# A hybrid RG-LRU / Conformer layer on one core: RMS row, gate and LayerNorm matmuls moved by a quarter or two, a fifth landing place for the squares of x, mean differences in small buffers

## The chip, the core and the metric

The kernel runs on one core of a Trainium2 chip. Its metric is device time in microseconds (us), median of three runs. TensorE (PE) does the matmuls, VectorE (DVE) and ScalarE (ACT) work on tiles in on-chip memory, GpSimd (POOL) and SyncE (SP) mostly issue transfers.

## What is computed

One layer over 1088 tokens (1024 of a prompt, 8 x 8 of a decode batch), all in float32:

```python
proj = rmsnorm(x) @ w_in                  # 2048 -> 5 x 1024
xa, ga, vb, gglu, gb = split(proj)
xc = dwconv4(xa)                          # causal, then block-diagonal gates
r, ig = sigmoid(xc @ gate_a + b), sigmoid(xc @ gate_x + b)
a = exp(-8 * r * softplus(-lru_param))
h = scan(a, sqrt(1 - a*a) * ig * xc)      # h[t] = a[t] h[t-1] + b[t]
ya = h * silu(ga)
u = vb * sigmoid(gglu)
yb = silu(layernorm(dwconv31(u))) * silu(gb)
y = rmsnorm(x + concat(ya, yb) @ w_out)   # and states h, conv tails
```

## The kernel before

Every float32 operand of a matmul is split into a rounded part `hi` and a rest `lo`, and each product is three matmuls (hi·hi, lo·hi, hi·lo). The projection runs over 40 column blocks of 128, in the `order` gg, vb, xa, ga for each of eight channel groups i (n = 4i to 4i+3), and then the eight gb blocks (n = 32 to 39). The first two blocks run together while x arrives, in eight units (`project_unit`, two values of k for both blocks). From n = 2 on, `project` runs a block in four quarters q of four values of k, one unit each. A unit is 32 matmuls. Each unit's weights are loaded by SP, split by ACT (L159) and DVE (L160) two units ahead, in a ring of three buffers.

`at(n, q, f)` puts f behind the unit of quarter q of block n (q of 4 and more counts on into later blocks), so f's matmuls stand in PE's queue there. Each engine's queue has a fixed order, written at build time by a planner that goes by place in the program: `tc.high_priority(URGENT)` moves the weight splits up by 200, `pump` moves the 31 taps of the long convolution (L412 to L416) and the mean update `stats` back by 400. An instruction whose input is late holds up all behind it on its engine.

The normalisation of x is folded in after the projection. `square_x` loads x by POOL into one of four borrowed places (two of tag "wmq", one "cb", one "sg") and ACT squares it, 18 times; `rms_stats` makes 1/rms, spreads it over a diagonal, splits that, and five pairs of small matmuls with ones (L363, L364) give the row `rstd`, which ACT copies out (L365). Blocks of n = 2 on need `rstd` to leave PSUM: `a_half` (xa), `first_b` (the first two blocks, parked in on-chip memory), `scaled`. PSUM has eight banks; a block takes three, a gate chunk two, each piece of the RMS row one.

For group i, `a_half` convolves xa in three chunks (`conv`, at the quarters `A_CONV`) and `a_chunk` runs six gate matmuls per chunk (at `A_GATE`). These use a ring of nine small buffers, `tt`. The product with silu(ga) goes to DRAM from a "sg" buffer, of which there are two. `stats` keeps a running mean of the long convolution's output over the groups: the difference `wd` goes into a "sg" buffer too, and `add_squares` squares it. In n = 33 and 34, `ln_mean` and `ln_rstd` sum over partitions with ones (L316, L317); `finish_b` applies the LayerNorm. The output projection follows.

Of the kernel before, what the change touches and what calls it, by code (L numbers as in the profile page):

```python
# [7 lines left out]
F32 = mybir.dt.float32  # L8
F32R = mybir.dt.float32r
# [20 lines left out]
LRU_C = 8.0  # L30
EPS = 1e-6

A_CONV = (0, 1, 3)
A_GATE = (2, 4, 6)
WARM = 8
URGENT = 200
LATER = 400
LN_AT = (0, 4, 6)
TAPS = {"xa": 3, "ga": 1, "gg": 2, "vb": 2}


# [22 lines left out]
def hybrid_layer_kernel(  # L64
# [135 lines left out]
    def project_unit(g, pts):  # L200

        hi, lo = wsplit.pop(g)
        wide, part, rest = [], [], []
        for m, (n, k) in enumerate(units[g]):
            ks = slice(m * P, (m + 1) * P)
            first, last = k == 0, k == NK - 1
            xh, xl = xs_[k]
            for src, w_t, fl, ll in ((xh, hi, first, False), (xl, hi, False, False), (xh, lo, False, last)):
                for c, (t0, tn, gr, go) in enumerate(CHUNKS[:2]):
                    to = wide if c == 0 else part  # L210
                    to.append((w_t is lo, pts[n][c][:, :tn], w_t[:, ks], src[gr][:, go : go + tn], fl, ll))

            t0, tn, gr, go = CHUNKS[2]
            both = xg_[k].rearrange("p (s t) -> p s t", s=2)[:, :, go : go + tn]
            pt = pts[n][2]
            wide.append(
                (False, pt[:, : 2 * tn].rearrange("p (s t) -> p s t", s=2), hi[:, ks], both, first, False)
            )
            rest.append((True, pt[:, :tn], lo[:, ks], xh[gr][:, go : go + tn], False, last))
        for group in (wide, part, rest):  # L220
            for _, out, w, mv, fl, ll in sorted(group, key=lambda z: z[0]):
                PE.matmul(out, w, mv, start=fl, stop=ll)  # L222

# [74 lines left out]
    squares = []  # L298

    def add_squares():  # L300
        for m, d in squares:
            S.activation(d, d, AF.Square, scale=float((m / (m + 1.0)) ** 0.5))
            V.tensor_add(wmq[1], wmq[1], d)
        squares.clear()

    def at(n, q, f):
        hooks.setdefault((n + q // NQ, q % NQ), []).append(f)


    def partition_sum(pt, src, c, name):  # L310

        t0, tn = ACH[c]
        hi, lo = tt(f"{name}h{c}", F32R), tt(f"{name}l{c}", F32R)
        S.copy(hi[:, :tn], src)
        V.tensor_sub(lo[:, :tn], src, hi[:, :tn].bitcast(F32))
        PE.matmul(pt[:, :tn], ones_r, hi[:, :tn], start=True, stop=False)  # L316
        PE.matmul(pt[:, :tn], ones_r, lo[:, :tn], start=False, stop=True)  # L317

    def square_x(n):

        t0, h = n // 2 * P, n % 2
        m = min(P, T - t0)

        if n % 4 < 2:
            xt = sp.tile([P, T], F32, tag="wmq", name=f"xt{n}", bufs=2)
        else:
            xt = full(*((("cb", f"xt{n}", 1), ("sg", f"xt{n}", 2))[n % 4 - 2]))
        if n < 2:

            G.tensor_copy(xt[:, :1], xs_[NK - 2 + n][0][0][:, :1].bitcast(F32))  # L330
        G.dma_start(xt[:m, : D // 2], x[t0 : t0 + m, h * (D // 2) : (h + 1) * (D // 2)])
        c = h * NT + n // 2
        S.activation(xt[:m, : D // 2], xt[:m, : D // 2], AF.Square, accum_out=ssx[:m, c : c + 1])

    def rms_stats():

        v, r, t = (sp.tile([P, NT], F32, name=f"rms{m}") for m in range(3))
        V.tensor_tensor(v, ssx[:, :NT], ssx[:, NT:], ALU.add)
        V.tensor_scalar(v, v, 1.0 / D, EPS, ALU.mult, ALU.add)
        S.activation(r, v, AF.Sqrt)  # L340
        V.reciprocal(r, r)
        refine(r, v, t)

        for n in range(0, NT, 2):
            t0 = n * P
            tn = min(2 * P, T - t0)
            c, o = divmod(t0, 512)
            nb = -(-tn // P)
            w = min(tn, P)
            dg, hi, lo = tt(f"dg{n}"), tt(f"dh{n}", F32R), tt(f"dl{n}", F32R)  # L350
            G.affine_select(
                out=dg[:, :tn].rearrange("p (b t) -> p b t", t=w),
                in_=r[:, n : n + nb].unsqueeze(2).to_broadcast([P, nb, w]),
                pattern=[[0, nb], [1, w]],
                base=0,
                channel_multiplier=-1,
                compare_op=ALU.is_equal,
                fill=0.0,
            )
            S.copy(hi[:, :tn], dg[:, :tn])  # L360
            V.tensor_sub(lo[:, :tn], dg[:, :tn], hi[:, :tn].bitcast(F32))
            pt = bank(f"rb{n}")
            PE.matmul(pt[:, :tn], ones_r, hi[:, :tn], start=True, stop=False)  # L363
            PE.matmul(pt[:, :tn], ones_r, lo[:, :tn], start=False, stop=True)  # L364
            S.copy(rstd[:, t0 : t0 + tn], pt[:, :tn])  # L365

    def full(tag, name, bufs):
        return ka.tile([P, T], F32, tag=tag, name=name, bufs=bufs)
# [34 lines left out]
    def b_conv(i, u, us):  # L403
        G.dma_start(o_bp[i], u[:, SEQ : SEQ + CB - 1])
        G.dma_start(o_bs[i].rearrange("p (b s) -> p b s", s=CB - 1), us[:, :, DS:])
        cb = full("cb", f"cb{i}", 1)
        cs = cb[:, SEQ:].rearrange("p (b s) -> p b s", s=DS)

        def tap(j):
            w = col(C_BW + j, i)  # L410
            if j == 0:
                V.tensor_scalar(cb[:, :SEQ], u[:, :SEQ], w, col(C_BB, i), ALU.mult, ALU.add)  # L412
                V.tensor_scalar(cs, us[:, :, :DS], w, col(C_BB, i), ALU.mult, ALU.add)
            else:
                V.scalar_tensor_tensor(cb[:, :SEQ], u[:, j : j + SEQ], w, cb[:, :SEQ], ALU.mult, ALU.add)  # L415
                V.scalar_tensor_tensor(cs, us[:, :, j : j + DS], w, cs, ALU.mult, ALU.add)  # L416

        def stats():
            G.dma_start(cbd[i], cb)
            wm, wq = wmq  # L420
            if i == 0:
                S.copy(wm, cb)
                G.memset(wq, 0.0)
                return
            d = full("sg", f"wd{i}", 2)
            V.tensor_sub(d, cb, wm)
# [131 lines left out]

    G.memset(ssx, 1.0)
    for n in range(2 * NT):  # L560
        at(2, n // 4, lambda n=n: square_x(n))
    at(2, 4, rms_stats)
    wmq = []
    at(2, 4, lambda: wmq.extend(sp.tile([P, T], F32, tag="wmq", name=f"wmq{m}", bufs=2) for m in range(2)))
    at(2, 2, softplus_consts)
    at(2, 6, first_b)

    conv = None
    for n, (kind, i, ct) in enumerate(order):
        if kind == "gb":  # L570
            break
        if n < 2:
            continue
        pts = project(n, TAPS[kind] if i < NC - 1 else 4)
        if kind == "gg":
            sg = full("sg", f"sg{i}", 2)
            scaled(sg, pts)
            b_gate(sg)
        elif kind == "vb":
            pump(len(bg))  # L580
            u, us = u_buffer(i)
# [47 lines left out]
    for n in range(4 * NC, 5 * NC):  # L629
        i = n - 4 * NC  # L630
        if i == 1:
            at(n, LN_AT[0], lambda: pump(len(bg)))
            at(n, LN_AT[0], add_squares)
            at(n, LN_AT[0], ln_mean)
            at(n, LN_AT[1], ln_rstd)
            at(n, LN_AT[2], lambda sg=sg0: finish_b(0, sg))
        if i > 1:
            at(n, LN_AT[2] - NQ, lambda i=i, sg=sg: finish_b(i - 1, sg))
        pts = project(n, 8)
        sg = full("sg", f"sgb{i}", 2)  # L640
        if i == 0:
# [266 lines left out]
```

## Time and profile before

| | |
|---|---|
| median of three runs | 1396.89 us (1396.36 to 1400.49) |
| the profiled execution | 1391.9 us |
| its span, first to last instruction | 1390.2 us |
| PE busy | 98% of the span |
| DVE busy | 69% |
| ACT busy | 39% |

The rows of the trace stand further below. Times are us from the start of the span. "Idle before <- releaser" is how long the engine stood still ahead of the instruction, and what ended that.

### The profile page before, as it was taken

The page shows a single profiled execution, that of the slowest core. Times are in us where ns is not written, and L with a number is a line of the kernel's source. Part 1 is how long each engine was busy: PE and PEld are TensorE (multiplying, and loading weights), DVE is VectorE, ACT ScalarE, POOL GpSimd, SP SyncE. Part 2 cuts the span into 40 slices and gives each one's busy share as a digit, 9 for nine tenths or more (in the row PEclk, how much of TensorE's full clock was granted, in tenths as well). Part 3 has the DMA queues.
Part 4 walks back from the last instruction along what each step waited for, and adds up shares of the span by engine and source line. Part 5 has one row for each costly group of instructions (what it writes and reads, how often), then busy time and mean ns, then how long its engine had stood idle before and what let it go on. Part 6 is the DMA issues. An engine that isn't in the chain of part 4 may idle for free.

```text
span 1390.2 us, 18376 instructions
## 1 busy us (share of the span) xinstructions
PE 1361.7 (98%) x6998; PEld 1185.9 (85%) x6998; DVE 954.1 (69%) x1625; ACT 546.4 (39%) x887; POOL 83.4 (6%) x153
## 2 busy tenths in 40 slices
PE   8989999999999999999999999999999999999997
PEld 7868888888888888888888898888888888888886
DVE  6359989798798796895996995843433463444342
ACT  6653617217227126126136164332333353333232
POOL 0210110100101001001001000000000000100000
PEclk9989999999999999999999999999999999999999
DMA  8831131321322313114123133343773356622333
GB/s 296 268 108 50 62 59 45 80 49 64 59 45 69 59 47 79 49 46 78 50 47 74 52 97 65 104 116 104 250 239 128 123 161 212 222 65 79 122 103 109
DMA packets 69129, 143.73 MB, mean 103 GB/s; under 512 B 9073, under 2 KB 12785, under 8 KB 68913
## 3 DMA queue, kind: packets, MB, share of 16 engines
q1 hardware_dynamic: 60032, 113.84, 28.0%
q0 software_dynamic: 8864, 28.72, 7.7%
q8 instruction: 54, 0.88, 0.3%
q14 instruction: 35, 0.28, 0.1%
q10 hardware_dynamic: 144, 0.01, 0.0%
HBM read 119.00 MB, written 23.54 MB: 103 GB/s over the span
## 4 chain that ended last, share of the span: by engine, by line
PE 58%; DVE 22%; ACT 7%; issue 6%; DMA 6%; POOL 1%; SPq 0%; DVEq 0%; ACTq 0%; POOLq 0%
PE pp L222 30%; DVE cb L415 9%; PE po L729 8%; PE po L728 8%; PE po L731 7%; DMA yd<-sga 3%; DVE wl L160 3%; DVE cb L416 3%; DMA xt<-in_x_dram 2%; DVE xc L464 2%; PE pz L729 1%; PE pz L728 1%; PE pz L731 1%; ACT L487 1%; ACT wh L159 1%
## 5 line engine op out<-in xcount | busy, mean ns | idle before, releaser
L222 PE MATMUL pp<-xg,wh 128*128 128x320 f32 (+1 forms) x1920 | 464.4, 336 | 1.9 <-DVE xg L194 1.9
L222 PEld LDWEIGHTS pp<-xg,wh 128*128 128x128 f32 x1920 | 321.7, 188 | 41.0 <-DVE xg L194 2.2
L415 DVE SCALAR_TENSOR_TENSOR cb<-u,prm,cb 128x1024 f32<-128x1024 f32 x240 | 307.1, 1280 | 1.6
L222 PE MATMUL pp<-xh,wh 128*128 128x512 f32 x640 | 252.7, 395 | 0.3 <-ACT xh L193 0.3
L222 PE MATMUL pp<-xl,wh 128*128 128x512 f32 x640 | 252.2, 394 | 0.3 <-DVE xl L194 0.3
L159 ACT CAST wh<-wr 128x512 fp32r<-128x512 f32 (+1 forms) x161 | 98.0, 612 | 279.8 <-DMA wr<-in_w_in_dram 130.0
L222 PE MATMUL pp<-xg,wl 128*128 128x256 f32 (+1 forms) x1280 | 196.3, 296 | 0.0
L222 PEld LDWEIGHTS pp<-xg,wl 128*128 128x128 f32 x1280 | 185.9, 189 | 0.0
L718 DVE TENSOR_TENSOR ol<-or,oh 128x512 fp32r<-128x512 f32 x114 | 78.5, 690 | 143.4 <-ACT oh L717 137.3
L222 PE MATMUL pp<-xh,wl 128*128 128x512 f32 x640 | 172.5, 391 | 1.0 <-DVE wl L160 0.9
L160 DVE TENSOR_TENSOR wl<-wr,wh 128x512 fp32r<-128x512 f32 (+1 forms) x161 | 109.9, 683 | 59.5 <-ACT wh L159 37.7
L222 PEld LDWEIGHTS pp<-xh,wl 128*128 128x128 f32 x640 | 119.5, 188 | 29.0 <-DVE wl L160 4.7
L222 PEld LDWEIGHTS pp<-xh,wh 128*128 128x128 f32 x640 | 121.8, 190 | 21.2 <-ACT xh L193 0.6
L222 PEld LDWEIGHTS pp<-xl,wh 128*128 128x128 f32 x640 | 121.6, 190 | 19.7 <-DVE xl L194 0.6
L717 ACT CAST oh<-or 128x512 fp32r<-128x512 f32 x114 | 70.6, 621 | 153.4 <-PE po L731 73.9
L729 PE MATMUL po<-ol,yh 128*128 128x512 f32 x256 | 99.8, 390 | 0.0
L728 PE MATMUL po<-oh,yh 128*128 128x512 f32 x256 | 99.7, 389 | 0.0
L731 PE MATMUL po<-oh,yl 128*128 128x512 f32 x256 | 99.7, 389 | 0.0
L729 PE MATMUL po<-ol,yg 128*128 128x512 f32 x240 | 93.6, 390 | 0.0
L728 PE MATMUL po<-oh,yg 128*128 128x512 f32 x240 | 93.5, 390 | 0.0
L731 PE MATMUL po<-oh,yg 128*128 128x512 f32 x192 | 74.8, 389 | 0.0
L416 DVE SCALAR_TENSOR_TENSOR cb<-u,prm,cb 128x64 f32<-128x64 f32 x240 | 67.7, 282 | 4.8
(217 smaller groups left out, 1466.2 us busy)
## 6 DMA issues: line engine op xcount, KB each, us to landing
wr<-in_w_in_dram SPq DMA_DIRECT2D x152, 256.0 KB, 3.0
or<-in_w_out_dram SPq DMA_DIRECT2D x128, 256.0 KB, 3.5
xt<-in_x_dram POOLq DMA_DIRECT2D x16, 512.0 KB, 5.5
xr<-in_x_dram SPq DMA_DIRECT2D x32, 256.0 KB, 3.1
xraw<-in_xT_dram SPq DMA_DIRECT2D x15, 544.0 KB, 6.1
yr<-yd SPq DMA_DIRECT2D x16, 288.0 KB, 2.8
cbd<-cb POOLq DMA_DIRECT2D x8, 544.0 KB, 3.9
yd<-sga POOLq DMA_DIRECT2D x8, 544.0 KB, 8.9
```

What stands on the lines that cost most here:

```text
L159: S.copy(hi[:, sl], raw[:, sl])
L160: V.tensor_sub(lo[:, sl], raw[:, sl], hi[:, sl].bitcast(F32))
L222: PE.matmul(out, w, mv, start=fl, stop=ll)
L415: V.scalar_tensor_tensor(cb[:, :SEQ], u[:, j : j + SEQ], w, cb[:, :SEQ], ALU.mult, ALU.add)
L416: V.scalar_tensor_tensor(cs, us[:, :, j : j + DS], w, cs, ALU.mult, ALU.add)
L464: V.scalar_tensor_tensor(o, src(j), col(C_AW + j, i), o, ALU.mult, ALU.add)
L487: S.activation(a[:, :tn], r[:, :tn], AF.Exp, scale=sp_n[:, i : i + 1])
L717: S.copy(hi, raw)
L718: V.tensor_sub(lo, raw, hi.bitcast(F32))
L728: PE.matmul(pt, yh, hi, start=k == 0, stop=False)
L729: PE.matmul(pt, yh, lo, start=False, stop=k == NK - 1 and yl is None)
L731: PE.matmul(pt, yl, hi, start=False, stop=k == NK - 1)
```

## The change

Six things. The quarters of the gate and LayerNorm work move: `A_CONV` (0, 1, 3) to (0, 1, 4), `A_GATE` (2, 4, 6) to (3, 5, 7), `LN_AT` from three places to five. The RMS row's matmuls leave `rms_stats` for `rms_row`, two quarters later, in three wide pieces where there were five; the diagonal and its split now live in "cb" and "wmq" buffers. `first_b` and the first `a_half` go a quarter later. The squares of x rotate through five places (the fifth is xa's buffer), five to a quarter. `stats` works on three chunks in `tt` buffers instead of one "sg" buffer. The first unit runs all of k = 0 ahead of k = 1. In LayerNorm, the split (`parts`) is issued a quarter ahead of the matmuls.

```diff
-A_CONV = (0, 1, 3)
-A_GATE = (2, 4, 6)
+A_CONV = (0, 1, 4)
+A_GATE = (3, 5, 7)
-LN_AT = (0, 4, 6)
+LN_AT = (0, 1, 3, 5, 7)
...
     def project_unit(g, pts):
-        wide, part, rest = [], [], []
-        for m, (n, k) in enumerate(units[g]):
+        blocks = list(enumerate(units[g]))
+        if g == 0:
+            for k in (0, 1):
+                project_blocks([b for b in blocks if b[1][1] == k], hi, lo, pts)
+        else:
+            project_blocks(blocks, hi, lo, pts)
...
-            wide.append(
+            (side if len(blocks) == 2 else wide).append(
...
-        for group in (wide, part, rest):
+        for group in (wide, side, part, rest):
...
     def add_squares():
-        for m, d in squares:
+        for m, d, sl in squares:
             S.activation(d, d, AF.Square, scale=float((m / (m + 1.0)) ** 0.5))
-            V.tensor_add(wmq[1], wmq[1], d)
+            V.tensor_add(wmq[1][:, sl], wmq[1][:, sl], d)
...
-        if n % 4 < 2:
+        m5 = n % 5
+        if m5 < 2:
             xt = sp.tile([P, T], F32, tag="wmq", name=f"xt{n}", bufs=2)
+        elif m5 < 4:
+            xt = full(*((("cb", f"xt{n}", 1), ("sg", f"xt{n}", 2))[m5 - 2]))
         else:
-            xt = full(*((("cb", f"xt{n}", 1), ("sg", f"xt{n}", 2))[n % 4 - 2]))
+            xt = kb.tile([P, AS + DB * AW], F32, tag="xa", name=f"xt{n}")
...
     def rms_stats():
+        dg = full("cb", "dg", 1)
+        dh, dl = (sp.tile([P, T], F32R, tag="wmq", name=f"d{m}", bufs=2) for m in "hl")
...
-            S.copy(hi[:, :tn], dg[:, :tn])
-            V.tensor_sub(lo[:, :tn], dg[:, :tn], hi[:, :tn].bitcast(F32))
-            pt = bank(f"rb{n}")
-            PE.matmul(pt[:, :tn], ones_r, hi[:, :tn], start=True, stop=False)
-            PE.matmul(pt[:, :tn], ones_r, lo[:, :tn], start=False, stop=True)
-            S.copy(rstd[:, t0 : t0 + tn], pt[:, :tn])
+            S.copy(dh[:, sl], dg[:, sl])
+            V.tensor_sub(dl[:, sl], dg[:, sl], dh[:, sl].bitcast(F32))
+        diag.extend((dh, dl))
+
+    def rms_row():
+        dh, dl = diag
+        for t0 in range(0, T, 512):
+            tn = min(512, T - t0)
+            sl = slice(t0, t0 + tn)
+            pt = bank(f"rb{t0}")
+            PE.matmul(pt[:, :tn], ones_r, dh[:, sl], start=True, stop=False)
+            PE.matmul(pt[:, :tn], ones_r, dl[:, sl], start=False, stop=True)
+            S.copy(rstd[:, sl], pt[:, :tn])
+        wmq.extend(sp.tile([P, T], F32, tag="wmq", name=f"wmq{m}", bufs=2) for m in range(2))
...
-            d = full("sg", f"wd{i}", 2)
-            V.tensor_sub(d, cb, wm)
-            V.scalar_tensor_tensor(wm, d, 1.0 / (i + 1), wm, ALU.mult, ALU.add)
-            squares.append((i, d))
+            for c, (t0, tn) in enumerate(ACH):
+                sl = slice(t0, t0 + tn)
+                d = tt(f"wd{i}_{c}")[:, :tn]
+                V.tensor_sub(d, cb[:, sl], wm[:, sl])
+                V.scalar_tensor_tensor(wm[:, sl], d, 1.0 / (i + 1), wm[:, sl], ALU.mult, ALU.add)
+                squares.append((i, d, sl))
...
-        at(2, n // 4, lambda n=n: square_x(n))
+        at(2, n // 5, lambda n=n: square_x(n))
     at(2, 4, rms_stats)
-    at(2, 4, lambda: wmq.extend(sp.tile([P, T], F32, tag="wmq", name=f"wmq{m}", bufs=2) for m in range(2)))
+    at(2, 6, rms_row)
     at(2, 2, softplus_consts)
-    at(2, 6, first_b)
+    at(2, 7, first_b)
...
-            at(n, 5, lambda n=n, i=i, pts=pts: a_half(n + 1, i, pts))
+            at(n, 6, lambda n=n, i=i, pts=pts: a_half(n + 1, i, pts))
...
-            at(n, LN_AT[0], ln_mean)
-            at(n, LN_AT[1], ln_rstd)
-            at(n, LN_AT[2], lambda sg=sg0: finish_b(0, sg))
+            at(n, LN_AT[0], lambda: ln_parts("lm", wm))
+            at(n, LN_AT[1], ln_mean)
+            at(n, LN_AT[2], lambda: ln_parts("lv", wq))
+            at(n, LN_AT[3], ln_rstd)
+            at(n, LN_AT[4], lambda sg=sg0: finish_b(0, sg))
```

## Rows read from the trace of the kernel before

**Rows 1.** The page, busy time: engine, us (share of span), instructions.
```profile
PE 1361.7 (98%) x6998; PEld 1185.9 (85%) x6998; DVE 954.1 (69%) x1625; ACT 546.4 (39%) x887; POOL 83.4 (6%) x153
```
**Rows 2.** Stretches: length, busy PE, PEld, DVE, ACT, POOL, clock, DMA share, GB/s.
```profile
15.44:80.20 64.76, 64.76 (x355) 57.66 (x353) 32.25 (x73) 42.84 (x78) 11.34 (x23) 1.00 0.83 270
86.09:103.92 17.83, 11.14 (x44) 8.97 (x43) 11.44 (x26) 10.47 (x21) 3.80 (x7) 0.71 0.18 47
...
213.86:710.48 496.62, 489.58 (x2653) 433.60 (x2651) 425.61 (x709) 188.53 (x275) 37.92 (x65) 1.00 0.26 58
...
710.48:807.64 97.16, 97.16 (x532) 86.82 (x531) 86.22 (x143) 44.21 (x64) 7.44 (x13) 1.00 0.25 59
833.12:884.91 51.79, 50.07 (x270) 43.71 (x269) 35.07 (x59) 20.62 (x33) 1.81 (x4) 1.00 0.24 57
```
**Rows 3.** What PE waited for: line, releaser, us in total, times, longest.
```profile
PE rb L363 <- ACT dh L360: 6.2, 1, 6.2
PE pr L482 <- DVE cl L468: 6.0, 5, 1.3
PE pp L222 <- DVE xg L194: 1.9, 1, 1.9
...
PE pp L222 <- DVE wl L160: 0.9, 3, 0.4
```
**Rows 4.** PE in order of time: start, us, line, idle before and its releaser.
```profile
80.20 0.40 PE L222 MATMUL pp<-xh,wh 128*128 128x512 f32 x1
80.43 0.40 PE L222 MATMUL pp<-xl,wh 128*128 128x512 f32 x1
...
92.44 0.58 PE L363 MATMUL rb<-dh,ones_r 128*128 128x256 f32 x1 [6.19 <-ACT dh L360]
...
95.35 0.58 PE L363 MATMUL rb<-dh,ones_r 128*128 128x256 f32 x1 [0.49 <-ACT rstd L365]
```
**Rows 5.** ACT in order of time, around the squares of x.
```profile
79.41 0.61 ACT L159 CAST wh<-wr 128x512 fp32r<-128x512 f32 x1
...
87.31 1.06 ACT L333 ACTIVATE xt<-xt 128x1024 f32<-128x1024 f32 x1 [4.70 <-DMA xt<-in_x_dram]
```
**Rows 6.** DVE in order of time, from the diagonal to the first u.
```profile
77.91 0.31 DVE L413 TENSOR_SCALAR cb<-u,prm 128x64 f32<-128x64 f32 x1 [7.76 <-ACT xt L333]
78.26 2.21 DVE L416 SCALAR_TENSOR_TENSOR cb<-u,prm,cb 128x64 f32<-128x64 f32 x7
...
80.99 4.77 DVE L416 SCALAR_TENSOR_TENSOR cb<-u,prm,cb 128x64 f32<-128x64 f32 x15
...
95.21 0.21 DVE L361 TENSOR_TENSOR dl<-dg,dh 128x64 fp32r<-128x64 f32 x1
95.60 0.69 DVE L442 TENSOR_TENSOR xa<-pp,rstd 128x512 f32<-128x512 f32 x1 [0.18 <-ACT rstd L365]
...
169.19 0.69 DVE L583 TENSOR_TENSOR u<-pp,sg 128x512 f32<-128x512 f32 x1
```
**Rows 7.** Groups by line and shape: count, busy us, mean ns, idle before them.
```profile
L426 DVE TENSOR_TENSOR wd<-cb,wmq 128x1088 f32<-128x1088 f32 x7 | 9.0, 1291 | 41.5 <-DMA yd<-sga 41.5
...
L604 DVE TENSOR_TENSOR ld<-wmq,lm 128x364 f32<-128x364 f32 x2 | 1.1, 534 | 0.1
```
**Rows 8.** Stretches: the loading of x, DVE's first round, and a later round.
```profile
43.00:71.00 28.00, 28.00 (x155) 24.96 (x154) 7.98 (x32) 18.89 (x39) 7.30 (x16) 1.00 0.86 284
...
98.00:172.00 74.00, 74.00 (x400) 66.05 (x399) 71.18 (x108) 37.73 (x52) 7.10 (x10) 0.98 0.17 47
...
362.00:461.00 99.00, 97.73 (x533) 86.84 (x532) 83.34 (x138) 38.66 (x56) 7.62 (x13) 1.00 0.27 59
```
**Rows 9.** The start: a stretch, and the second unit's first use of x block 3.
```profile
7.40:10.90 3.50, 2.49 (x6) 2.02 (x7) 2.31 (x3) 1.49 (x3) 0.00 (x0) 0.62 0.91 303
...
15.67 0.81 DVE L194 SCALAR_TENSOR_TENSOR xg<-xraw,ng,xg 128x576 fp32r<-128x576 f32 x1
...
16.83 0.39 PE L222 MATMUL pp<-xg,wh 128*128 128x512 f32 x1
```

More of the change, by code (lines that the diff above doesn't have):

```diff
@@ L202, in project_unit, with project_blocks @@
         hi, lo = wsplit.pop(g)
-        wide, part, rest = [], [], []
-        for m, (n, k) in enumerate(units[g]):
+        blocks = list(enumerate(units[g]))
[4 more added lines that the diff above has]
+            project_blocks(blocks, hi, lo, pts)
+    def project_blocks(blocks, hi, lo, pts):
+        wide, side, part, rest = [], [], [], []
+        for m, (n, k) in blocks:
             ks = slice(m * P, (m + 1) * P)
@@ L307, in at, with parts, partition_sum @@
         hooks.setdefault((n + q // NQ, q % NQ), []).append(f)
[L310 to L315, printed above, removed]
-        PE.matmul(pt[:, :tn], ones_r, hi[:, :tn], start=True, stop=False)
-        PE.matmul(pt[:, :tn], ones_r, lo[:, :tn], start=False, stop=True)
+    def parts(src, name):
+        out = []
+        for c, (t0, tn) in enumerate(ACH):
+            sl = slice(t0, t0 + tn)
+            hi, lo = tt(f"{name}h{c}", F32R)[:, :tn], tt(f"{name}l{c}", F32R)[:, :tn]
+            S.copy(hi, src[:, sl])
+            V.tensor_sub(lo, src[:, sl], hi.bitcast(F32))
+            out.append((hi, lo))
+        return out
+    def partition_sum(pt, part):
+        tn = part[0].shape[-1]
+        PE.matmul(pt[:, :tn], ones_r, part[0], start=True, stop=False)
+        PE.matmul(pt[:, :tn], ones_r, part[1], start=False, stop=True)
     def square_x(n):
@@ L342, in rms_stats @@
         refine(r, v, t)
-        for n in range(0, NT, 2):
-            t0 = n * P
+        dg = full("cb", "dg", 1)
+        dh, dl = (sp.tile([P, T], F32R, tag="wmq", name=f"d{m}", bufs=2) for m in "hl")
+        for t0 in range(0, T, 2 * P):
             tn = min(2 * P, T - t0)
[L347 to L350, printed above, removed]
+            n, nb, w = t0 // P, -(-tn // P), min(tn, P)
+            sl = slice(t0, t0 + tn)
             G.affine_select(
-                out=dg[:, :tn].rearrange("p (b t) -> p b t", t=w),
+                out=dg[:, sl].rearrange("p (b t) -> p b t", t=w),
                 in_=r[:, n : n + nb].unsqueeze(2).to_broadcast([P, nb, w]),
@@ L359, in rms_stats @@
             )
-            S.copy(hi[:, :tn], dg[:, :tn])
-            V.tensor_sub(lo[:, :tn], dg[:, :tn], hi[:, :tn].bitcast(F32))
-            pt = bank(f"rb{n}")
-            PE.matmul(pt[:, :tn], ones_r, hi[:, :tn], start=True, stop=False)
-            PE.matmul(pt[:, :tn], ones_r, lo[:, :tn], start=False, stop=True)
-            S.copy(rstd[:, t0 : t0 + tn], pt[:, :tn])
+            S.copy(dh[:, sl], dg[:, sl])
+            V.tensor_sub(dl[:, sl], dg[:, sl], dh[:, sl].bitcast(F32))
+        diag.extend((dh, dl))
+    diag = []
+    def rms_row():
+        dh, dl = diag
+        for t0 in range(0, T, 512):
+            tn = min(512, T - t0)
+            sl = slice(t0, t0 + tn)
+            pt = bank(f"rb{t0}")
[3 more added lines that the diff above has]
+        wmq.extend(sp.tile([P, T], F32, tag="wmq", name=f"wmq{m}", bufs=2) for m in range(2))
     def full(tag, name, bufs):
@@ L424, in stats @@
                 return
-            d = full("sg", f"wd{i}", 2)
-            V.tensor_sub(d, cb, wm)
-            V.scalar_tensor_tensor(wm, d, 1.0 / (i + 1), wm, ALU.mult, ALU.add)
-            squares.append((i, d))
+            for c, (t0, tn) in enumerate(ACH):
+                sl = slice(t0, t0 + tn)
+                d = tt(f"wd{i}_{c}")[:, :tn]
+                V.tensor_sub(d, cb[:, sl], wm[:, sl])
+                V.scalar_tensor_tensor(wm[:, sl], d, 1.0 / (i + 1), wm[:, sl], ALU.mult, ALU.add)
+                squares.append((i, d, sl))
         for j in range(CB):
@@ L594, in hybrid_layer_kernel, with ln_parts @@
     wm, wq = wmq
+    lnp = {}
+    def ln_parts(name, src):
+        lnp[name] = parts(src, name)
     def ln_mean():
@@ L600, in ln_mean @@
             pt = bank(f"lm{c}")
-            partition_sum(pt, wm[:, sl], c, "lm")
+            partition_sum(pt, lnp["lm"][c])
             d = tt(f"ld{c}")
@@ L612, in ln_rstd @@
             pv = bank(f"lv{c}")
-            partition_sum(pv, wq[:, sl], c, "lv")
+            partition_sum(pv, lnp["lv"][c])
             v, t = tt(f"lw{c}"), tt(f"lt{c}")
@@ L633, in hybrid_layer_kernel @@
             at(n, LN_AT[0], add_squares)
-            at(n, LN_AT[0], ln_mean)
-            at(n, LN_AT[1], ln_rstd)
-            at(n, LN_AT[2], lambda sg=sg0: finish_b(0, sg))
+            at(n, LN_AT[0], lambda: ln_parts("lm", wm))
[3 more added lines that the diff above has]
+            at(n, LN_AT[4], lambda sg=sg0: finish_b(0, sg))
         if i > 1:
-            at(n, LN_AT[2] - NQ, lambda i=i, sg=sg: finish_b(i - 1, sg))
+            at(n, LN_AT[4] - NQ, lambda i=i, sg=sg: finish_b(i - 1, sg))
         pts = project(n, 8)
```

## The prediction

> **What bounds the kernel now.** I read the busy times first, then PE's waits, then stretches of whole units, then the queues around each loss. PE is busy 98% of the span, DVE 69%, ACT 39% [rows 1]. So the kernel can become faster only where PE stands still or runs at half clock. The eleven units from 15.44 to 80.20 us show the undisturbed pace: 64.76 / 11 = 5.887 us a unit at clock 1.00 [rows 2]. A unit's start is seen by its 512-column matmul of xh with wh, and 512 columns take 80.43 - 80.20 = 0.23 us [rows 4]. The last of the seven full rounds of four blocks, 710.48 to 807.64, takes 97.16 us: 16 units (94.19) and 18 gate matmuls (2.97, so 0.165 each), and PE is busy all of it [rows 2]. That is the reference for the other rounds. PE's list of waits names where time is lost: the RMS row behind `dh`, the gates behind `cl`, some weight rests, and the start [rows 3]. A wait's own length is less than what it costs, so I take costs from the stretches.
>
> **The RMS row.** Unit n = 3, q = 0 starts at 80.20 and ends at 86.09; the unit after next starts at 103.92. The 17.83 us between hold one unit (5.887), hence 11.94 are wait, half clock (mean 0.71) and the row's own ten matmuls [rows 2]. PE was idle 6.19 us before the first of them, because ACT's `dh` came late [rows 4], and it came late because the last square of x began at 87.31 after 4.70 us of waiting for its load [rows 5]. The clock fell to its 1.2 GHz level while PE stood. After the change, `rms_row` stands behind n = 3, q = 2: PE asks at 80.20 + 3 x 5.887 = 97.86. The last `dl` was done at 95.21 + 0.21 = 95.42 [rows 6], so even with squares no earlier than now PE has 2.4 us to spare. The new row is four 512-column and two 64-column matmuls, 4 x 0.23 and about 0.07 each for the small ones: 1.06. Gain 11.94 - 1.06 = 10.9 us. Only two of eight PSUM banks are free for three pieces, so the third waits for ACT's copy of the first; the same wait was 0.49 at 95.35 [rows 4]. I charge 0.5.
>
> **The rounds.** Five rounds, 213.86 to 710.48, take 496.62 us; five undisturbed ones would take 5 x 97.16 = 485.80. So 10.8 us are lost there [rows 2], by two causes: the first gate chunk waits for `cl` (five times, up to 1.3 us, 6.0 in all), and weight rests come late behind a stalled DVE [rows 3]. That stall is `wd`, whose "sg" buffer is still being sent to DRAM: 41.5 us of idle over the seven groups [rows 7]. The change moves the first two gate chunks a unit further from their convolution, 5.887 us against a lack of 1.3, and keeps the third chunk's distance of three quarters, which showed no wait. It takes `wd` out of the "sg" buffers altogether. I count the whole 10.8. What is late next would be DVE itself, but it is busy 83.34 of 99 us in such a round [rows 8], and loses waits of 41.5 / 7, some 6 us. The cost: three pieces instead of one for each of three DVE instructions. A 364-column piece takes 0.53 and the whole 1.29 [rows 7], so 3 x (1.60 - 1.29) = 0.9 us of DVE a round, hidden by the 15 idle. If that cover were gone it would be 7 x 0.9 = 6.5 us.
>
> **LayerNorm.** Blocks 33 and 34 take 51.79; eight units are 47.10 and twelve sums at 0.165 are 2.0, so 2.7 are lost [rows 2]. With the split issued a quarter (5.9 us) ahead of the sums I count 2.7 back. `finish_b` goes a quarter later, on DVE and ACT, which are half idle there (35.07 and 20.62 of 51.79); nothing on PE waits for it before the output projection's row block k = 14. I count 0.
>
> **The first unit.** PE waited 1.9 us for `xg` [rows 3], and 7.40 to 10.90 ran at a mean clock of 0.62 [rows 9]. By k, there is more work before that wait. But the second unit takes x block 3 at 16.83, and DVE finished that at 15.67 + 0.81 = 16.48 [rows 9]: the feed, not PE, sets the time from there. At most the parts of the second unit that need only block 2 move up. Bounds: a gain of 1.5 (most of the 1.9), a loss of 1.7, if PE, done sooner and waiting more, is granted the half clock for one more such stretch of 3.5 us. I take 0, the end nearest to the row of the feed.
>
> **The squares.** Five places let one more load be under way. They count for nothing by themselves, since the row is asked for at 97.86 anyway; what they touch is ACT's queue (rival B). DVE's first round is the edit with a price: the 23 decode taps that DVE did early, from 77.91 to 85.76 (7 us without the weight split), need "cb", now held by the diagonal until about 95. In the kernel before, from the first xa (95.60) to the first u of the next group (169.19), 73.6 us passed [rows 6], and DVE was busy 71.18 of the 74 us there [rows 8]. After, xa starts 2 to 3.2 us behind 97.86 (3.2 was 95.60 - 92.44), so the first u comes at 173.5 to 174.7, or up to 181.7 with all decode taps behind it. Block n = 7 begins at 97.86 + 1.06 + 13 x 5.887 + 18 x 0.165 = 178.4 and its third matmul needs a bank that this u frees, 0.7 later. So a wait of 0 to 3.5; I take 1.0, since DVE's idle time around 87 to 95 can take most of the taps.
>
> **Sum.** 10.9 + 10.8 + 2.7 = 24.4, less 0.5 and 1.0, is 22.9 us. The profiled execution took 1391.9 (span 1390.2 and 1.7 around it), 5.0 under the median of 1396.89; all the losses counted are waits inside the program, so I take the difference over unchanged: 1369.0 profiled, 1396.9 - 22.9 = 1374.0 for the median.
>
> **The rivals.** *B: ACT's queue jams at the squares.* The split of the weights for n = 3, q = 0 ended at 79.41 + 0.61 = 80.02 [rows 5], the unit began at 80.20 [rows 4]: 0.2 us to spare, since the cast stood behind squares that waited for loads. If the planner counts on five places and the loads don't come faster, more squares stand before that cast. In the worst case it stands behind the last square, at 88.4 + 0.6: PE waits 9 and half clock adds 4, as it now does after the row's wait. Half of it is 6.5, with the row's own wait of some 2.5 on top 9: 1383. For it: the loads ran at 284 GB/s with the DMA engines 0.86 busy [rows 8], so at most 1 / 0.86 = 1.16 times faster. Against: a share of 0.86 leaves some room, and the squares' places in the program move up by as much as a quarter, so the last come earlier.
>
> The Trainium skill (DMA: Bandwidth & Descriptors, Specifications) gives a limit of about 358 GB/s from HBM for a core. The trace's 284 lies under it; by the page loads could be 358 / 284 = 1.26 times faster, not 1.16, and B's chance would be nearer 0.12 than 0.16. The sum is the same by either.
>
> *C: the gates still wait.* DVE, not the distance, sets `cl`, and its lag grows with PE's gain: the gates' part stays, 10.8 less five late weight rests of about 0.7, some 7.3: 1381. Against it: DVE loses a stall of some 6 us a round ahead of that point.
>
> *D: the planner puts the row's sums where they were,* and the change does not do what it says there: 10.9 stay, 1385. In the kernel before they stood exactly behind their unit, so I give it little.
>
> *E: slower.* The nine `tt` buffers become the bound. A gate chunk uses up to eight, `wd` now three from `stats` to `add_squares`; if the next convolutions or gates wait for these, DVE stalls every round. DVE has about 15 us idle a round, so PE loses nothing until such waits pass some 15; to be 0.3% slower than before they must take back 22.9 + 4.2 = 27.1, or 3.9 in each of seven rounds, so waits of 19 us, three times the 6 that `wd` waits now. That would give 1402. Against it: `wd` comes after the chunks of its group are done.
>
> **Chances and range.** Forecast 0.66 (1369 to 1379), B 0.16, C 0.07, D 0.03, B at its full price of 13 to 16 and C together 0.04 (about 1396), E 0.04. About 0.3%, 4.2 us, is what a measurement here can tell from no change. Faster: 0.66 + 0.16 + 0.07 + 0.03 = 0.92; same 0.04; slower 0.04. The range takes in the forecast with its bounds (24.4 and the start's 1.5 give 1371, less 2 for the spread of runs) and B, C and D: 1369 to 1386.
>
> **What would show it.** Right: the wait for `dh` is gone and the clock stays 1.00 from 86 to 104; rounds of 97.2 us; no wait for `cl`; `wd` no longer behind a transfer; LayerNorm's two blocks near 49.1. Wrong: PE waiting for `wh` between 57 and 98 (B), for `cl` (C), for a bank at the start of n = 7 (my 1.0 too small), or DVE waiting for small buffers (E).

## The result, and the profile after

The changed kernel takes 1377.44 us (median; 1375.39 to 1380.23), the kernel before beside it 1397.41 (1396.36 to 1400.49; one run more than in the table above): 20.0 us less, ratio 0.9855, 95% interval [0.9831, 0.9878]. Later, beside the experiments, the changed kernel took 1374.36 and the one before 1392.01, 17.7 apart (1392.0 to 1393.0 beside the other kernels). The forecast was 1374.0, a gain of 22.9. The two profiled executions have spans of 1390.2 and 1373.7, so 16.5 us apart; the sum below is made against these.

The page of after, busy time, and what PE waited for (line, releaser, us in total, times, longest), against [rows 1, 3]:

```profile
PE 1354.6 (99%) x6994; PEld 1181.8 (86%) x6994; DVE 950.7 (69%) x1667; ACT 553.8 (40%) x902; POOL 80.5 (6%) x153
```

```profile
PE pr L512 <- ACT ch L498: 3.0, 2, 2.4
PE pp L230 <- DVE xg L194: 1.3, 1, 1.3
...
PE pr L513 <- DVE cl L499: 0.8, 1, 0.8
PE px L512 <- DVE sga L407: 0.8, 1, 0.8
PE po L766 <- ACT oh L755: 0.6, 2, 0.3
PE po L767 <- DVE ol L756: 0.4, 2, 0.2
```

The wait of 6.2 for `dh` is gone, and of the five waits for `cl`, 6.0 in all, one of 0.8 is left, at another place. New at the top is `ch`, the rounded part of a convolution chunk, ahead of a gate.

Stretches of after (length, busy PE, PEld, DVE, ACT, POOL, clock, DMA share, GB/s): n = 3, q = 1 to the start of n = 4; the five rounds n = 8 to 27; the round after them; n = 33 and 34; and the loading of x:

```profile
84.83:103.66 18.83, 18.83 (x104) 16.61 (x103) 16.56 (x44) 7.75 (x15) 2.29 (x4) 1.00 0.20 58
201.79:694.39 492.60, 487.62 (x2651) 433.84 (x2651) 440.18 (x764) 197.12 (x293) 36.19 (x65) 1.00 0.28 59
694.39:791.54 97.15, 97.15 (x532) 86.81 (x531) 84.38 (x146) 39.76 (x59) 6.75 (x13) 1.00 0.27 59
817.02:866.51 49.49, 49.38 (x270) 43.83 (x269) 31.36 (x56) 24.16 (x38) 2.14 (x4) 1.00 0.27 55
43.00:71.00 28.00, 28.00 (x153) 24.76 (x152) 7.61 (x30) 19.51 (x41) 8.23 (x16) 1.00 0.93 311
```

Against [rows 2, 8]: the row's half clock is gone (1.00, PE busy 18.83 of 18.83), the LayerNorm blocks came down from 51.79 to 49.49, but the five rounds only from 496.62 to 492.60, where 485.8 is the undisturbed time. The loss of 6.8 us that is left there is what the experiments are about. In order of time:

| stretch | before | after | gain |
|---|---|---|---|
| start of unit n = 3, q = 0 | 80.20 | 78.94 | 1.26 |
| from there to n = 4 | 35.50 | 24.72 | 10.78 |
| n = 4 to 7 | 98.16 | 98.13 | 0.0 |
| five rounds, n = 8 to 27 | 496.62 | 492.60 | 4.0 |
| the round n = 28 to 31 | 97.16 | 97.15 | 0.0 |
| n = 33 and 34 | 51.79 | 49.49 | 2.3 |
| the rest, the output projection above all | | | -1.9 |

The last row is lost at the waits of PE for `oh` and `ol` at 1295 and 1309 us, in code that the change doesn't touch; in the executions of the experiments' kernels below the same stretch is between 0.3 shorter and 0.7 longer than before's.

The RMS row in after: the last piece of `dl` on DVE, the first decode taps, and the sums on PE (start, us, engine, line, idle before and its releaser):

```profile
86.37 0.23 DVE L379 TENSOR_TENSOR dl<-dg,dh 128x64 fp32r<-128x64 f32 x1 [0.16 <-ACT dh L378]
87.45 0.30 DVE L442 TENSOR_SCALAR cb<-u,prm 128x64 f32<-128x64 f32 x1
87.79 5.10 DVE L445 SCALAR_TENSOR_TENSOR cb<-u,prm,cb 128x64 f32<-128x64 f32 x16
```

```profile
96.60 0.39 PE L391 MATMUL rb<-dh,ones_r 128*128 128x512 f32 x1
...
97.99 0.21 PE L391 MATMUL rb<-dh,ones_r 128*128 128x64 f32 x1
```

The reader is to see that the sums wait for nothing, with 10 us between 86.60 and 96.60.

Where the rounds still lose. On DVE the first tap of the second group's long convolution (L441) and the first small tap of the third (L442) wait for a transfer. POOL issued that transfer, `cbd` from `cb`, 3 us ahead of `yd` from "sga", both 544 KB; the third view is the DMA issues from 160 to 190 us (KB each, us from issue to landing):

```profile
180.06 0.81 DVE L441 TENSOR_SCALAR cb<-u,prm 128x1024 f32<-128x1024 f32 x1 [8.80 <-DMA cbd<-cb]
...
264.65 0.31 DVE L442 TENSOR_SCALAR cb<-u,prm 128x64 f32<-128x64 f32 x1 [6.42 <-DMA cbd<-cb]
```

```profile
168.63 0.55 POOL L448 DMA_DIRECT2D cbd<-cb  x1
...
171.65 0.54 POOL L559 DMA_DIRECT2D yd<-sga  x1 [0.17 <-issue]
```

```profile
cbd<-cb POOLq DMA_DIRECT2D x1, 544.0 KB, 11.3
yd<-sga POOLq DMA_DIRECT2D x1, 544.0 KB, 10.4
```

`cb` has one buffer. So from 171.3 to 180.06 DVE, whose queue is in order, does nothing, in a round that keeps it busy nearly all the time: from 180 to 227 it is busy 46.9 of 47 us, so it can't catch up. The end of the chain is seen in the second group's gates: DVE's square step (`q`) of the first gate chunk, its scan, which frees small buffers, the third convolution, ACT's `ch`, and PE, which asked for `ch` too early; then the same place a group later:

```profile
218.24 0.53 DVE L522 SCALAR_TENSOR_TENSOR q<-q,r 128x364 f32<-128x364 f32 x1
222.52 0.90 DVE L534 TENSOR_TENSOR_SCAN h<-a,ig 128x364 f32<-128x364 f32 x1
223.34 0.41 DVE L493 TENSOR_SCALAR xc<-xa,prm 128x296 f32<-128x296 f32 x1
```

```profile
226.60 0.49 ACT L498 CAST ch<-xc 128x360 fp32r<-128x360 f32 x1 [6.79 <-DVE xc L495]
```

```profile
227.15 0.43 PE L512 MATMUL pr<-ch,gh 128*128 128x360 f32 x1 [0.61 <-ACT ch L498]
...
329.83 0.43 PE L512 MATMUL pr<-ch,gh 128*128 128x360 f32 x1 [2.37 <-ACT ch L498]
```

### The profile page after: what moved, and what is told of

It reads as the page before. It is cut to its first block, busy times and chain, and to the rows that moved or that the text cites. A ratio compares the mean times of both kernels' runs of the same rounds, so it can differ in the third digit from the quotient of the medians.

```text
span 1373.7 us, 18413 instructions
## 1 busy us (share of the span) xinstructions
PE 1354.6 (99%) x6994; PEld 1181.8 (86%) x6994; DVE 950.7 (69%) x1667; ACT 553.8 (40%) x902; POOL 80.5 (6%) x153
## 4 chain that ended last, share of the span: by engine, by line
PE 84%; DVE 11%; DMA 4%; issue 1%; ACT 1%; POOL 0%; SPq 0%; ACTq 0%; DVEq 0%; POOLq 0%
PE pp L230 57%; PE po L767 7%; PE po L766 7%; PE po L769 7%; DVE cb L444 5%; DMA or<-in_w_out_dram 2%; DMA cbd<-cb 2%; PE pz L766 1%; PE pz L767 1%; DVE wl L160 1%; PE pz L769 1%; DVE cb L445 1%; DVE xc L495 1%; DMA xraw<-in_xT_dram 0%; DVE ol L756 0%
## 5 line engine op out<-in xcount | busy, mean ns | idle before, releaser
L230 PEld LDWEIGHTS pp<-xh,wh 128*128 128x128 f32 x640 | 120.7, 189 | 21.9 <-ACT xh L193 1.3
```

## The experiments

Each was run beside the kernel before, and ratios are to that. "Lost in the rounds" is the length of the five rounds less 485.8; before 10.8, after 6.8.

**The changed kernel again** (after_again), unaltered, beside four of the kernels below.

> The changed kernel once more, as the measure for the runs beside it. The third gate chunk of groups 1 and 2 is again the one that PE waits for; five rounds of groups 2 to 6 at 492 to 493 us; about 20 us shorter than the kernel before.

Measured: 1374.36, ratio 0.9882 [0.9851, 0.9913]; rounds 493.49. The same waits at the same places. After the one at 329.8 this execution shows a stretch at half clock, which the first didn't:

```profile
331.60:335.10 3.50, 3.50 (x10) 2.78 (x9) 1.20 (x2) 3.44 (x6) 0.00 (x0) 0.52 0.19 56
```

**wd alone** (b_wd). The kernel before with the mean difference in three small buffers, all else as it was.

```diff
-            d = full("sg", f"wd{i}", 2)
-            V.tensor_sub(d, cb, wm)
-            ...
+            for c, (t0, tn) in enumerate(ACH):
+                sl = slice(t0, t0 + tn)
+                d = tt(f"wd{i}_{c}")[:, :tn]
+                V.tensor_sub(d, cb[:, sl], wm[:, sl])
+                ...
```

> The kernel before with one part of the change alone: the mean difference in three small buffers. Theory wd: the transfer that wd waited for was what made DVE late at the first gate chunk and at the weight rests, so with gates at their old quarters the five rounds of groups 2 to 6 take 486 to 488 us instead of 496.6 and the time falls by 9 to 11 us; the RMS row's and LayerNorm's waits stay. Rival distance: the gates need their later quarter; only the weight rests' part comes back, 2 to 4 us.

Measured: 1379.39, ratio 0.9909 [0.9892, 0.9925]: 12.6 us less than the 1392.01 beside it. Its five rounds, its two LayerNorm blocks (n = 33 and 34), and its longest wait of PE:

```profile
213.96:699.85 485.89, 485.89 (x2652) 433.97 (x2651) 438.30 (x750) 201.40 (x296) 35.12 (x65) 1.00 0.27 60
822.58:872.19 49.61, 49.61 (x270) 43.73 (x269) 35.13 (x59) 21.73 (x34) 1.80 (x4) 1.00 0.30 55
```

```profile
PE rb L363 <- ACT dh L360: 5.1, 1, 5.1
```

The rounds lose nothing, with the gates at their old quarters. So the whole 10.8 were `wd`'s transfer, the waits for `cl` too: the gates' distance wasn't at fault. Some 2.2 us more come from the LayerNorm blocks, 49.61 for 51.79, though their sums stand in the old order here. `rms_stats` still costs nearly what it cost: 35.00 us from n = 3 to n = 4, for 35.50.

**wd back in "sg"** (e_wdsg), in the changed kernel.

```diff
-            for c, (t0, tn) in enumerate(ACH):
-                ...
+            d = full("sg", f"wd{i}", 2)
+            V.tensor_sub(d, cb, wm)
+            ...
```

> The changed kernel with the mean difference wd back in one sg buffer (all else as changed). If the small buffers freed DVE from the transfer of sga, that wait comes back with some 41 us over the groups, weight rests come late again, and the five rounds of groups 2 to 6 take 3 to 6 us more than 492.6; time 3 to 6 us longer. If the later gates alone did the work, wd's wait comes back without cost to PE and the time is within 1 us of the changed kernel's.

Measured: 1399.04, ratio 1.0051 [1.0035, 1.0067], slower than before by 0.5%, and 24.7 us behind the changed kernel, where 3 to 6 were expected. DVE's group of `wd` (count, busy, mean ns, idle before), the five rounds, and n = 33 and 34:

```profile
L455 DVE TENSOR_TENSOR wd<-cb,wmq 128x1088 f32<-128x1088 f32 x7 | 9.0, 1291 | 50.9 <-DMA yd<-sga 50.9
```

```profile
201.73:710.38 508.65, 495.30 (x2651) 438.96 (x2651) 418.79 (x706) 191.47 (x278) 36.84 (x65) 0.99 0.23 56
840.91:890.24 49.33, 49.33 (x270) 43.81 (x270) 30.88 (x55) 23.06 (x35) 2.08 (x4) 1.00 0.33 55
```

22.9 us are lost in the rounds, and 7.9 more in the round after them (105.03 for 97.15 in after): the rest of the change makes `wd`'s wait dearer (50.9 for 41.5 of [rows 7]), and PE's waits with it. LayerNorm, with its split issued early, takes 49.33 even so.

**The same with the gates at their old quarters** (e_wdsg_gold).

```diff
-A_CONV = (0, 1, 4)
-A_GATE = (3, 5, 7)
+A_CONV = (0, 1, 3)
+A_GATE = (2, 4, 6)
```

> The kernel after with two edits: the mean difference back in one "sg" buffer, and the gates at their old quarters. It stands against the run with the "sg" buffer alone (1399.0), which lost some 30 us in the rounds, with wd idle 51 us behind the transfer of ya. Theory 1 (the later gates send ya off later, so wd meets the transfer later): the wait of wd falls back to about 41 us, the five rounds from n = 8 to n = 28 come back to about 497 us as in the kernel before, and the time is 1378 to 1384. Theory 2 (the longer backlog on DVE that the later RMS row leaves makes the wait costly): the rounds stay above 505 us and the time is 1390 to 1399.

Measured: 1371.57, ratio 0.9855 [0.9836, 0.9874], 27 us under the last one and better than either theory said.

```profile
202.10:692.52 490.42, 487.59 (x2652) 433.67 (x2651) 430.57 (x722) 188.35 (x274) 40.27 (x65) 1.00 0.26 59
```

So it was the later gates, not the later row, that made `wd`'s wait dear. `wd` still waits for the transfer, 33.9 us in four, and the rounds lose 4.6.

**The old quarters, with wd in small buffers** (e_gates_old): the same diff on the changed kernel.

> The changed kernel with the convolutions and gates at their old quarters (0, 1, 3 and 2, 4, 6). If the later gates removed the first chunk's wait for cl, it comes back: some 1.5 us in each of five groups, and the third chunk's waits in groups 2 and 3 stay; time 5 to 9 us longer than the changed kernel's. If freeing DVE from the sga transfer did that, cl is in time at the old places too and the time is within 2 us of the changed kernel's.

Measured: 1366.92, ratio 0.9818 [0.9804, 0.9833], 7.4 less than the changed kernel again, which neither theory said; and nothing lost in the rounds:

```profile
202.32:688.02 485.70, 485.70 (x2652) 433.96 (x2651) 442.10 (x760) 197.78 (x290) 39.53 (x65) 1.00 0.27 60
```

**The row a quarter earlier** (e_early), with the first blocks and the first convolution.

```diff
-    at(2, 6, rms_row)
+    at(2, 5, rms_row)
-    at(2, 7, first_b)
+    at(2, 6, first_b)
-            at(n, 6, lambda n=n, i=i, pts=pts: a_half(n + 1, i, pts))
+            at(n, 5, lambda n=n, i=i, pts=pts: a_half(n + 1, i, pts))
```

> The changed kernel with the RMS row, the first xa block and the first gated block one quarter earlier (behind n = 3, q = 1 and 2). Theory backlog: the third gate chunk waits for its convolution in the second and third group only because DVE starts its first round late and has no idle time until the fourth; starting it 5.9 us earlier leaves PE's waits in the five rounds of groups 2 to 6 at 0 to 3 us instead of 6.8 (492.6 us for 80 units becomes 486 to 489), the row is still not waited for (its operands were ready 10 us before the sums), and the time falls by 3 to 6 us. Rival ring: the convolution waits for small buffers that the first gate chunk holds, whatever DVE does; the five rounds stay at 492 to 493 us.

Measured: 1367.07, ratio 0.982 [0.9805, 0.9834], 7.3 less than the changed kernel again, where 3 to 6 were expected, and the rounds lose nothing, though the gates are at the late quarters:

```profile
202.56:688.38 485.82, 485.82 (x2652) 434.03 (x2651) 433.33 (x748) 197.25 (x290) 37.70 (x65) 1.00 0.26 60
```

At this point it looked as if DVE's later first round and the later gates each had a share. The next run was to see whether the two gains add.

**Both: the old quarters and the earlier row** (e_both).

> The kernel after with the gates at their old quarters and the RMS row, first_b and the first convolution a quarter earlier: each of the two alone gave 1367. Theory 1 (both took away the same waits, in the second and third round): nothing is left to gain there, rounds of 97.2 us, 1366 to 1368. Theory 2 (each took away a loss of its own): the two gains of some 7 us add, and the time is 1359 to 1362.

Measured: 1374.12, ratio 0.988 [0.986, 0.9899]: as slow as the changed kernel, which neither theory said. Two edits that each took away the loss bring it back together (rounds 491.51). A story of distances alone doesn't fit that, so the question became what DVE waits for. The first tap of the second group in three kernels, e_both, the old quarters and the earlier row; and, for e_both, two issues of POOL:

```profile
182.84 0.81 DVE L441 TENSOR_SCALAR cb<-u,prm 128x1024 f32<-128x1024 f32 x1 [14.14 <-DMA cbd<-cb]
```

```profile
176.87 1.50 DVE L441 TENSOR_SCALAR cb<-u,prm 128x1024 f32<-128x1024 f32 x1 [4.05 <-DMA cbd<-cb]
```

```profile
167.92 0.81 DVE L441 TENSOR_SCALAR cb<-u,prm 128x1024 f32<-128x1024 f32 x1 [2.35 <-DMA cbd<-cb]
```

```profile
176.53 0.86 POOL L434 DMA_DIRECT2D out_o_bs_dram<-u  x1 [6.88 <-DMA u<-in_st_b_dram]
177.31 0.62 POOL L448 DMA_DIRECT2D cbd<-cb  x1
```

In e_both POOL issues the transfer of `cb` only at 177.31, since a store of the conv state ahead of it in POOL's queue waits for a load. In the kernel with the earlier row `yd` goes out 13 us behind `cbd`, at 177.30 and 163.80, and `cbd` landed 4.0 us after its issue:

```profile
cbd<-cb POOLq DMA_DIRECT2D x1, 544.0 KB, 4.0
yd<-sga POOLq DMA_DIRECT2D x1, 544.0 KB, 9.6
```

**The transfer from ACT's copy** (e_wm). The first group's result is copied by ACT into `wm` anyway; send it from there, and `cb` is free after the copy. Only that is changed against after:

```diff
-            G.dma_start(cbd[i], cb)
             wm, wq = wmq
+            G.dma_start(cbd[i], cb) if i else S.copy(wm, cb)
             if i == 0:
-                S.copy(wm, cb)
+                G.dma_start(cbd[i], wm)
```

> The kernel after with one transfer changed: the first group's long convolution is sent to DRAM from wm, ACT's copy of it, and not from cb, so the first tap of the second group waits for ACT's copy alone. In the kernel after DVE stands 8.8 us there (171.3 to 180.1) for that transfer, in the one round in which it has no slack. Theory 1 (this wait puts DVE behind, and the third gate chunks of the second and third group pay for it): the wait is 1 us or none, the rounds from n = 8 to n = 28 come down from 492.6 to about 486, and the time from 1374.4 to 1367, in [1365, 1369]. Theory 2 (the wait only fills time that DVE would lose anyway; the later gates are the cause): the rounds stay at 491 to 493 and the time is 1372 to 1376.

Measured: 1366.87, ratio 0.9818 [0.9801, 0.9834], as theory 1 had it. The first tap starts 8.8 us earlier than in after, with no idle before it; the square step and the third convolution of the second group, at 218.24 and 223.34 in after, come 8.4 and 8.0 earlier; and the rounds are at their undisturbed pace with gates and row where the change put them:

```profile
171.30 0.80 DVE L441 TENSOR_SCALAR cb<-u,prm 128x1024 f32<-128x1024 f32 x1
...
209.85 0.55 DVE L522 SCALAR_TENSOR_TENSOR q<-q,r 128x364 f32<-128x364 f32 x1
...
215.39 0.67 DVE L493 TENSOR_SCALAR xc<-xa,prm 128x296 f32<-128x296 f32 x2
```

```profile
201.91:687.60 485.69, 485.69 (x2651) 434.01 (x2651) 432.77 (x751) 197.31 (x291) 35.76 (x65) 1.00 0.26 60
```

The transfer itself got no quicker (9.3 us, beside `yd`'s 8.6); it only holds nobody any more. So without that wait the 6.8 us are not lost: this shows their cause.

The wait alone isn't enough, though: in b_wd it is as long and costs nothing. What goes with the loss is how long after the start of n = 4 on PE the second group's first tap starts on DVE. In b_wd, the old quarters, the earlier row and this kernel, which lose nothing in the rounds n = 8 to 15, that is 63.5 to 72.7 us; in after, e_both, e_inplace, e_four and e_u0old, which lose 3.8 to 9.0 there, it is 76 to 78.

**The same transfer in the kernel with both edits** (e_both_wm).

> The kernel with the gates at their old quarters and the row a quarter earlier (1374.1), with the same transfer changed. There DVE stands 14.1 us at that place, because POOL issues the transfer only at 177.3, behind another one that waits. Theory 1 (that wait is what the two edits together brought): it goes, the gate waits at 197, 297 and 303 us go with it, and the time is 1365 to 1368. Theory 2 (the two edits spoil each other in another way, by DVE's order): the time stays at 1371 to 1375.

Measured: 1369.65, ratio 0.9839 [0.9819, 0.9859]: 4.5 of the 7 are back, less than theory 1 said. The waits at 197 are gone; one of 1.3 and one of 0.7 at 293 are left, and 2.4 lost in the rounds. DVE waits once more for `cbd`, a group later:

```profile
254.32 0.31 DVE L442 TENSOR_SCALAR cb<-u,prm 128x64 f32<-128x64 f32 x1 [5.56 <-DMA cbd<-cb]
```

The kernel of the last experiment, e_wm, shows nearly the same wait, 5.52 at 254.39, without a loss. DVE also waits 5.46 us at 174.77 here, behind the first tap (166.55), for the load of the conv state, which that kernel doesn't, so here the place of the first tap, 62.6 us after the start of n = 4, doesn't tell of the loss; whether that wait is the rest, or DVE's order with the two edits, wasn't taken apart.

**Small buffers: the scan written over its input** (e_inplace), so that a gate chunk takes seven buffers of the ring, not eight.

```diff
-        r, ig, a, q, h = (tt(f"{nm}{i}_{c}") for nm in ("r", "ig", "a", "q", "h"))
+        r, ig, a, q = (tt(f"{nm}{i}_{c}") for nm in ("r", "ig", "a", "q"))
+        h = ig
```

> The changed kernel with the scan written over its own input, so that a gate chunk holds seven small buffers instead of eight; no instruction is added or taken away. Theory ring: the third convolution's first instruction no longer waits for the scan of the first chunk, starts 5 us or more earlier in every group, and the five rounds of groups 2 to 6 take 486 to 488 us instead of 492.6. Theory backlog: the buffers come free in time in groups 4 to 7 anyway, DVE's queue is as full as before in groups 2 and 3; the five rounds stay at 491 to 493.

Measured: 1369.14, ratio 0.983 [0.9814, 0.9847]. DVE waits for `cbd` about as long as in after (7.20 and 7.88, for 8.80 and 6.42), but the rounds lose 3.8 in place of 6.8, between the two theories. So the ring carries some of the delay on to PE; it doesn't make it. A ring of more buffers wasn't tried.

**Four places for the squares** (e_four).

```diff
-        m5 = n % 5
+        m5 = (0, 1, 2, 3)[n % 4]
...
-        at(2, n // 5, lambda n=n: square_x(n))
+        at(2, n // 4, lambda n=n: square_x(n))
```

> The changed kernel with the squares of x in four places, as before. If the later place of the row's sums is what removed its wait, the diagonal's rest is ready by about 91 to 95 us, the sums at 97 to 98 still wait for nothing, and the time is within 1.5 us of the changed kernel's. If the fifth place carries it, PE waits 2 us or more ahead of the sums or of the weights of n = 3 and the clock falls again: 4 to 12 us longer.

Measured: 1376.34, ratio 0.989 [0.9873, 0.9908], against 0.9882 [0.9851, 0.9913] for five. The sums still wait for nothing at first; the third piece shows the bank wait that the prediction charged:

```profile
98.10 0.39 PE L391 MATMUL rb<-dh,ones_r 128*128 128x512 f32 x1
...
100.08 0.30 PE L391 MATMUL rb<-dh,ones_r 128*128 128x64 f32 x1 [0.43 <-ACT rstd L393]
```

One wait of 1.0 at 60.4 (PE for ACT's copy at L579, which stands among the squares), which makes its unit 1.3 longer, is the only loss of the rival B's kind in any run. The last `dl` is done at 91.4, 6.7 us ahead of the sums. So the later place of the row, not the fifth buffer, took away the 6.2.

**The first unit in its old order** (e_u0old).

```diff
-        if g == 0:
-            for k in (0, 1):
-                project_blocks([b for b in blocks if b[1][1] == k], hi, lo, pts)
-        else:
-            project_blocks(blocks, hi, lo, pts)
+        project_blocks(blocks, hi, lo, pts)
```

> The changed kernel with the first unit in its old order. If the order by k moved the start, the third unit begins 0.5 to 1.3 us later than in the changed kernel (at 20.8 to 21.4 us) and a stretch of half clock stands between 8 and 12 us again; time 0.5 to 1.5 us longer. If the feed of x alone sets the start, the third unit begins within 0.2 us of the changed kernel's and the time is the same.

Measured: 1377.88, ratio 0.9898 [0.9878, 0.9918]; the interval overlaps that of after, so only the trace can speak. The third unit starts at 21.81 us, in after at 20.08 and in after again at 20.68, and the half clock of [rows 9] is back:

```profile
8.80:12.30 3.50, 3.49 (x9) 2.91 (x10) 1.48 (x2) 1.47 (x3) 0.00 (x0) 0.51 0.99 357
```

The other traces agree: in the three executions with the old order (before, b_wd and this one) a stretch at half clock begins between 8.2 and 9.0 us and the third unit at 21.3 to 21.9; in the eleven with the new order there is no such stretch, and the third unit begins at 20.0 to 21.3.

## Why the prediction was right, and where it was not

**The RMS row: right,** 10.9 less 0.5 forecast, 10.78 measured. The wait for a bank, priced at 0.5, did not come in after (0.43 with four places). The spare time was larger than the 2.4 of the prediction, 10 us. Of that the fifth place gave some 3: with it the loads ran at 311 GB/s, not 284 [rows 8], and the last square started at 79.2, not 87.3; with four places (278 GB/s, last square at 83.9) there were still 6.7. The rest came with the other edits and wasn't taken apart.

**The rounds: the term that was mis-sized.** Forecast 10.8, measured 4.0. Two steps of it were wrong. "The change moves the first two gate chunks a unit further" took the distance for one of two causes; b_wd shows that `wd` alone was the whole of it; with `wd` in small buffers the later gates bought nothing, and taking them back made the changed kernel 7.4 faster. And "What is late next would be DVE itself" was answered with DVE's mean share (83.34 of 99), which doesn't see the first rounds. The row's gain lets PE begin n = 4 at 103.66, not 115.70, but the first tap of the second group stayed where it was: 180.68 before, 180.06 after. DVE was thus 76.4 us behind that point, where it had been 65.0, and the wait for `cbd`, 7.56 before and 8.74 in b_wd, whose rounds lost nothing, cost 6.8 in after. In the trace of before that wait is one row, which the prediction didn't read, since it looked at DVE's waits by their sum, where `wd` stands out. That row, and the same in b_wd:

```profile
180.68 0.81 DVE L412 TENSOR_SCALAR cb<-u,prm 128x1024 f32<-128x1024 f32 x1 [7.56 <-DMA cbd<-cb]
```

```profile
181.95 0.81 DVE L412 TENSOR_SCALAR cb<-u,prm 128x1024 f32<-128x1024 f32 x1 [8.74 <-DMA cbd<-cb]
```

**LayerNorm: right in size, with a cause too few.** 2.7 forecast, 2.3 measured; 0.4 is left in the quarter of the first sums, where PE waits for `lml` once more (0.11 at 831.3). But the prediction put all of it down to the earlier split, and b_wd has the old split and takes 49.61, e_wdsg the new split with `wd` waiting and takes 49.33. Either edit alone brings the time back; the loss in the kernel before (51.79) needed `wd`'s wait as well as the late split.

**The first unit: a little too low.** Taken at 0 between -1.7 and 1.5; measured 1.26 in after's trace, within the bounds, and 1.1 between after again and the old order. The prediction had the feed alone set the time from there; the half clock had a share. The gain goes with the half clock that isn't granted in the new order: `xg` is still waited for, 1.3 us in after, but the clock stays at 1.00. That it stays because more of PE's work comes ahead of that wait is argued, not shown.

**DVE's first round: right in sign of the risk, wrong in its place.** Charged 1.0 at the start of n = 7; no such wait: the first u came at 168.40, not 173.5 to 174.7. The 23 decode taps ran from 87.45 to 95.3 in DVE's idle time, so they added nothing; the sums began at 96.60, not 97.86; xa began 1.3 us behind that (97.89), not 2 to 3.2; and from there to the first u it took 70.5 us, not 73.6. The lateness came out 60 us further on, in the gates.

**The sum** in the spans: 10.78 + 4.0 + 2.3 + 1.26 = 18.4, less 1.9 in the output projection, is 16.5, against 22.9. The median went down by 20.0, closer to the forecast than the traces are, because the profiled execution of before lay 5.5 under its median and that of after 2.0. Beside the experiments the medians lay 17.7 apart. So of the near hit in the median some 3 us are luck of the runs shown.

**The rivals.** B did not come, but for the 1.3 in e_four. D did not: the sums stood where the change put them. C was right in its rule, that DVE's lag grows with PE's gain; that it was near in size (7.3 kept, 6.8 measured) is chance, since its place was not `cl` of the first chunk but the third chunk, and only in the second and third group. E's ring did hand the delay on, at a few us, far from its 27 (whose time is 1374.0 + 27.1 = 1401, not 1402).

Three versions stand at 1366.9 to 1367.1 and beat both kernels: the old quarters, the earlier row, and the transfer from `wm`. In the last PE stands idle 3.2 us up to the third unit and 0.3 from there to 1350 us, so little is left to win by order alone.

## What to carry to other kernels

When a change takes a long wait from the engine that bounds, look at what that wait had hidden: the other engine's lag grows by nearly as much (11.4 us here, for 12.0 of PE), and its small waits on buffers that are being sent away begin to count, in the first rounds first. Read the waits of the second busiest engine row by row in those rounds, not by their sum over the run. A buffer with one copy should not be held by a transfer if another copy of the data exists.

## What the runs showed of the hardware

How long a 544 KB store holds its buffer varied by more than a factor of three. In after, two of them issued 3 us apart landed after 11.3 and 10.4 us; in the kernel with the earlier row `cbd` landed after 4.0. It isn't the other large store that sets this: in after the `yd` issued at 352.83 had no other large store within 27 us and took 9.8, and with the old quarters `yd` and `cbd`, issued 1.6 us apart at 169.77 and 171.41, took 4.9 and 5.3:

```profile
yd<-sga POOLq DMA_DIRECT2D x1, 544.0 KB, 9.8
```

```profile
yd<-sga POOLq DMA_DIRECT2D x1, 544.0 KB, 4.9
cbd<-cb POOLq DMA_DIRECT2D x1, 544.0 KB, 5.3
```

What goes with a slow landing in the fourteen traces is a store of 0.5 KB, the last column of h (`out_o_hp_dram`), which POOL issues at the end of each group's gates. Of the 224 stores of `cbd` and `yd` from "sga", the 90 that weren't in flight together with it took 3.5 to 6.1 us, and 130 of the 134 that were took 7.6 to 12.7; the other four took 3.8 to 5.9. No run leaves that store out or moves it alone, so that it is the cause isn't shown.

A wait of 2.4 us on PE at 329.8 was followed by a stretch at half clock in one execution (0.52 over 3.5 us) and not in the other of the same kernel (1.00 in the same stretch, where PE began 17 matmuls, not 10). The round's loss there was 1.6 us larger (the waits around 329.8 cost 4.63 in the one, 3.04 in the other, by the starts of the matmuls). The same wait of 2.37 in e_u0old was followed by half clock too, and in e_four it wasn't.
